# Delta-rule layer of a decoder trunk: the substitution's scratch, one tile for the lower blocks, and the place of the decays' product and the norms in GpSimd's queue

## The chip, the cores and the metric

The kernel runs on one core of a Trainium2 chip. A core has TensorE (matmuls; PE in the profile, PEld for its weight loads), VectorE (DVE), ScalarE (ACT), GpSimd (POOL) and SyncE (SP, which here only issues DMAs). Each engine runs its own queue of instructions in order; engines wait for one another through semaphores. The metric is the device time of one execution in microseconds, the median of several runs. A profiled execution is one run with the hardware profiler on; its page and its trace are what is quoted here.

## The reference

The program is a decoder trunk of four pre-norm residual layers (pooling mixer, gated DeltaNet, latent attention, pooling mixer) for 256 tokens and a model width of 1024, in float32. The change lies in the second layer, the delta rule. Cut to what matters:

```python
q = l2norm(q) * (GDN_DK ** -0.5);  k = l2norm(k)
g = cumsum(-exp(a_log) * softplus(a_raw + dt_bias))      # within a chunk
L = where(strict, (k_beta @ k.T) * decay, 0)
A = eye(C) + L
sol = triangular_solve(A, [v_beta, k_beta * exp(g)], lower=True)
attn = where(causal, (q @ k.T) * decay, 0)
for chunk in chunks:                                     # scan with a state
    v_new = u_c - w_c @ state
    o = (q_c * exp(g_c)) @ state + attn_c @ v_new
    state = state * exp(g_last) + k_dec.T @ v_new
o = rmsnorm(o, norm_g) * silu(gate)
```

There are 8 heads, keys of width 128 and values of width 256. The kernel takes chunks of 128 tokens instead of 64, so there are two (`NT` = 2).

## The kernel before

All large products run on TensorE from weights that are streamed from memory: SyncE loads a unit of a weight matrix into `raw` (line 104), ScalarE rounds it to the part `whi` (line 114), VectorE, or GpSimd for a few units, takes the difference `wlo` (line 119), and TensorE multiplies both with the activations (lines 128 to 130 and 169). This stream runs through the whole kernel and keeps TensorE busy; the rest of each layer is fitted beside it.

A framework traces the program, chooses the places of all tiles in the on-chip memory, plans the order of each engine's queue from a model of the durations, and sets the semaphores. Tiles of one tag (`s4` for the big ones) have no fixed places: a tile is put on bytes that an earlier tile has left, and its first writer then waits for that tile's last reader. `later(ins)` keeps what is traced inside it behind `ins` on the same engine's queue.

The delta layer's steps are listed by hand in line 561: `g0 k0 d a0 k1 a1 s g1 q0 v0 v1 v2 q1 V3 i c3 g2 u0 u1 g3`. In words: gates (`g`, the silu gate's projection), keys of four heads each (`k0`, `k1`), decays (`d`, exponentials of the tiles DT, Eb and eG), the lower-triangular blocks (`a`, into the two tiles `LT`), the substitution (`s`), queries (`q0`, `q1`), values (`v0` to `v3`; the fourth is split into its projection `V3` and its rest `c3`), the inverses (`i`) and the first chunk's new values (`u`).

The steps that matter:

- `substitution` (lines 717 to 751). The 32 by 32 diagonal blocks of `LT` (for 2 chunks, 8 heads and 4 blocks: 64 of them) are copied to DRAM by eight DMAs of SyncE's queue (line 723) and read back with one block on each of 64 partitions, `Lb` (line 728). GpSimd then solves all 64 at once, 31 pairs of a product into the scratch `pr` (line 733) and a difference into `Tb` (line 737). The result goes to DRAM (line 740) and back to the diagonal blocks of `T` by four DMAs of GpSimd's queue (line 744), each for one of the four blocks of all heads. VectorE and GpSimd also prepare factors here (lines 746 to 750).
- `queries(hf)` (lines 755 to 770). `channels` projects four heads, runs the short convolution (lines 635 and 638) and a silu into the tile `kqT`, that is `qT[hf]` (line 674), and turns it for the norms (line 680). `against` multiplies with the keys (line 693) and writes the masked scores (line 697). Then GpSimd multiplies the decays by the queries (`ev`, line 765) and computes the norms (lines 766 to 770); all of this stands in `later(mark["blocks"])`, and `mark["blocks"]` is the last difference of line 737.
- `inverses` (lines 806 to 857) stands in `later(mark["strip"], mark["dve"])` (line 881), that is behind the last matmul of `V3` on TensorE and behind the last split of a weight on VectorE. It turns the blocks T into the tiles `U` (line 817), reuses `Lb` and `Tb` as `X1` (memset in line 816), and combines blocks to full inverses in `pairs` (lines 826, 832) and `whole` (lines 840 to 853), four small batches of matmuls for each chunk. The first product of `pairs` (line 826) reads the first and the third block column of T (`blocks(T[t], 0)`).
- After that come `news` (line 867) and the outputs of each head (lines 892 to 956), which read the norms (lines 925 to 928).

Of the kernel before, what the change touches and what calls it, by code (L numbers as in the profile page):

```python
# [13 lines left out]
ALU = mybir.AluOpType  # L14
AX = mybir.AxisListType

P = 128
D = 1024
S = 256
NT = S // P  # L20
# [22 lines left out]
def trunk(ctx: ExitStack, tc: tile.TileContext, x, positions, norm_g, pool_w_in, pool_w_grp,  # L43
          pool_scale, pool_w_out, gdn_w_in, gdn_conv, gdn_a_log, gdn_dt_bias, gdn_norm_g,
          gdn_w_out, mla_w_in, mla_q_norm_g, mla_w_uq, mla_kv_norm_g, mla_w_ukv, mla_w_out,
          final_g, out, depth=4, final=True):
    nc = tc.nc
# [22 lines left out]
    def big(name, *dims, dt=F32):  # L70
        return s4.tile([P, *dims], dt, tag="s4", name=name)
# [7 lines left out]
    def small(name, *dims, bufs=2):  # L79
        return sm.tile([P, *dims], F32, tag=name, name=name, bufs=bufs)  # L80
# [12 lines left out]
    mark = {}  # L93
# [443 lines left out]
    def gdn_layer(i, j, hT):  # L537
        H = GDN_H
        M = NT * H
# [34 lines left out]
        for t in range(NT):  # L574
# [8 lines left out]
                                in1=dtb[:, None, :].to_broadcast([P, NT, H]))  # L583
# [13 lines left out]
                                in1=alog[:, None, :].to_broadcast([P, NT, H]))  # L597
# [14 lines left out]
        for t in range(NT):  # L612
            nc.gpsimd.dma_start(
                out=Gb[t].rearrange("p h s -> p (h s)"),
                in_=d_g[t * H:(t + 1) * H, :].rearrange("(a h) s -> a (h s)", a=1).to_broadcast(
                    [P, H * P]))
# [26 lines left out]
        Q, B = 4, 32  # L643
        Tb_ = big("Tb", B, B)
        Tb = Tb_[:M * Q]
        free = []
        nc.gpsimd.memset(Tb, 0.0)
        nc.gpsimd.memset(Tb.rearrange("m r c -> m (r c)")[:, ::B + 1], 1.0)
        Ts = big("T", NT, H, P)
# [4 lines left out]
        kT, qT = [], []  # L654
# [43 lines left out]
                    out=dst[t][:, h, :], in0=ps[:, b], scalar=sf[:, t, h:h + 1],  # L698
                    in1=DT[t][:, h, :], op0=ALU.mult, op1=ALU.mult)

        LT = [big("LT", H, P) for _ in range(NT)]

        def keys(hf):
            hs = slice(4 * hf, 4 * hf + 4)
# [8 lines left out]
        def lower(hf):  # L713
            for t in range(NT):
                against(LT, kT, s2, hf, t)

        def substitution():

            d_l = dram.tile([M * Q, B * B], F32, name="d_l")
            lv = d_l.rearrange("(t m d) (r c) -> t d r m c", t=NT, d=Q, r=B)  # L720
            for t in range(NT):
                for d in range(Q):
                    nc.sync.dma_start(out=lv[t, d],
                                      in_=LT[t][d * B:(d + 1) * B, :, d * B:(d + 1) * B])
            Lb_ = big("Lb", B, B)
            Lb = Lb_[:M * Q]
            free.extend((Lb_, Tb_))
            nc.sync.dma_start(out=Lb, in_=d_l.rearrange("m (r c) -> m r c", r=B))
            pr = small("pr", 256, bufs=1)[:M * Q]
            for r in range(B - 1):  # L730
                n, c = B - 1 - r, r + 1
                pv = pr[:, :n * c].rearrange("m (a b) -> m a b", a=n)
                nc.gpsimd.tensor_tensor(out=pv, op=ALU.mult,  # L733
                                        in0=Lb[:, r, r + 1:, None].to_broadcast([M * Q, n, c]),
                                        in1=Tb[:, r:r + 1, :c].to_broadcast([M * Q, n, c]))
                tv = Tb[:, r + 1:, :c]
                mark["blocks"] = nc.gpsimd.tensor_tensor(out=tv, in0=tv, in1=pv,  # L737
                                                         op=ALU.subtract).ins
            d_t = dram.tile([M * Q, B * B], F32, name="d_t")
            nc.gpsimd.dma_start(out=d_t.rearrange("m (r c) -> m r c", r=B), in_=Tb)  # L740
            tv = d_t.rearrange("(m d) (r c) -> d r m c", d=Q, r=B)
            for d in range(Q):
                dd = slice(d * B, (d + 1) * B)
                nc.gpsimd.dma_start(out=Ts[dd, :, :, dd].rearrange("p t h c -> p (t h) c"),
                                    in_=tv[d])
            nc.vector.reciprocal(rki, rk)
            nc.vector.tensor_tensor(out=kds, in0=rk[:, 0, :], in1=DT[0][:, :, P - 1],
                                    op=ALU.mult)
            nc.vector.tensor_scalar(neG, eG[:, 1, :], -1.0, None, ALU.mult)
            nc.gpsimd.tensor_tensor(out=ktok, in0=ktok, op=ALU.mult,  # L750
                                    in1=kds[:, :, None].to_broadcast([P, H, P]))
# [3 lines left out]
        def queries(hf):  # L755
            if hf == 0:
                at_.extend(big("attnT", H, P) for _ in range(NT))
            channels(qT, 0, hf, 1)
            for t in range(NT):
                against(at_, qT, rk, hf, t)  # L760
            ev = Eb[:, 4 * hf:4 * hf + 4, :]
            rh, qh = rq[:, :, 4 * hf:4 * hf + 4], rq2[:, :, 4 * hf:4 * hf + 4]

            with later(mark["blocks"]):
                nc.gpsimd.tensor_tensor(out=ev, in0=ev, in1=qT[hf][:, :, P:], op=ALU.mult)
                nc.gpsimd.tensor_scalar(qh, ssq[:, 1, :, 4 * hf:4 * hf + 4], float(P), EPS * P,
                                        ALU.mult, ALU.add)
                power(rh, qh)
                nc.gpsimd.tensor_tensor(out=qh, in0=rh, in1=rh, op=ALU.mult)
                nc.gpsimd.tensor_scalar(qh, qh, 1.0 / DV, None, ALU.mult)  # L770
# [29 lines left out]
            values_in(vi)  # L800
            values_done(vi)

        U = []
        u1 = []

        def inverses():
# [2 lines left out]

            U.extend(big("U", H, P) for _ in range(NT))

            X1 = [a.rearrange("p (h a) c -> p h (a c)", h=H) for a in free]
            for t in range(NT):
# [462 lines left out]
```

## Time and profile before

| | before |
|---|---|
| runs, us | 863.2, 864.64, 864.9 |
| median, us | 864.64 |
| profiled execution, us | 861.29 |
| its span, us | 859.5 |
| mean granted TensorE clock | 0.988 |
| DMA read from memory | 137.79 MB |

The span is the time between the first and the last instruction of the profiled execution; the 1.8 us around it are launch and end. The page gives for each engine how long it was busy, 40 slices of the span with the busy share of each engine, the granted TensorE clock in tenths of full speed, the DMA queues, the chain of work that ended last, and the costliest groups of instructions. The trace behind it can be asked for the instructions of an engine in order of time (start, duration, engine, line, operation, output and inputs, and in brackets how long the engine stood idle before it and what released it), for who waited for whom (total, times, longest, all in us), and for the busy time of each engine in stretches of the span.

### The profile page before, as it was taken

How to read it: one execution, taken by the hardware profiler on the slowest of the kernel's cores; microseconds unless marked ns; L12 is line 12 of the kernel's file. 1: busy time of each engine (PE TensorE's matmuls, PEld its weight loads, DVE VectorE, ACT ScalarE, POOL GpSimd, SP SyncE). 2: the span in 40 equal slices, each digit the busy share in tenths (PEclk: the TensorE clock that was granted, in tenths of full speed). 3: DMA queues.
4: the chain of work that ended last, by engine and by line, in shares of the span. 5: the costliest groups of instructions: out<-in, count | busy, mean ns of one | idle time of the engine just before them, and what ended most of it. 6: DMA issues, size and time to landing. Idle time of an engine off the chain costs nothing.

```text
span 859.5 us, 15387 instructions
## 1 busy us (share of the span) xinstructions
PE 834.2 (97%) x5967; PEld 780.0 (91%) x5967; DVE 568.4 (66%) x904; ACT 458.0 (53%) x757; POOL 168.5 (20%) x295
## 2 busy tenths in 40 slices
PE   7999999999999969999999999999999999999996
PEld 5999998979899968788989998999989979999986
DVE  4579866467889746355566557677767657766852
ACT  5555554466856634355455553566545465455542
POOL 4011000333338971022212003000000111100012
PEclk9999999999999979999999999999999999999999
DMA  5766657646556524303636676653552547566651
GB/s 196 228 197 192 203 171 224 193 122 205 168 172 194 172 76 144 124 26 104 190 108 220 203 174 191 172 149 97 151 171 80 159 148 217 182 188 183 205 184 50
DMA packets 109233, 140.37 MB, mean 163 GB/s; under 512 B 21228, under 2 KB 51112, under 8 KB 109160
## 3 DMA queue, kind: packets, MB, share of 16 engines
q1 hardware_dynamic: 106800, 137.65, 52.9%
q0 software_dynamic: 528, 1.58, 0.6%
q8 instruction: 47, 0.77, 0.4%
q10 hardware_dynamic: 1832, 0.16, 0.2%
q14 instruction: 26, 0.21, 0.1%
HBM read 137.79 MB, written 1.58 MB: 162 GB/s over the span
## 4 chain that ended last, share of the span: by engine, by line
PE 76%; POOL 7%; DMA 5%; DVE 5%; issue 3%; ACT 2%; SPq 0%; POOLq 0%; ACTq 0%; DVEq 0%
PE acc L169 32%; PE acc L130 10%; PE acc L129 10%; PE acc L128 10%; DMA raw<-in_pool_w_in_dram 3%; POOL pr L733 3%; POOL Tb L737 2%; PE aux L128 2%; PE aux L129 2%; PE aux L130 2%; DVE wlo L119 2%; ACT whi L114 1%; DMA raw<-in_mla_w_out_dram 1%; DVE cv L638 1%; PE aux L867 1%
## 5 line engine op out<-in xcount | busy, mean ns | idle before, releaser
L119 DVE TENSOR_TENSOR wlo<-raw,whi 128x1024 fp32r<-128x1024 f32 (+1 forms) x257 | 309.2, 1207 | 191.8 <-ACT whi L114 190.2
L114 ACT CAST whi<-raw 128x1024 fp32r<-128x1024 f32 (+2 forms) x258 | 265.3, 1032 | 245.8 <-PE acc L169 95.0
L129 PE MATMUL acc<-hTl,whi 128*128 128x256 f32 x832 | 235.1, 283 | 0.0
L130 PE MATMUL acc<-hTh,wlo 128*128 128x256 f32 x832 | 234.8, 283 | 0.0
L128 PE MATMUL acc<-hTh,whi 128*128 128x256 f32 x832 | 234.5, 282 | 0.0
L129 PEld LDWEIGHTS acc<-hTl,whi 128*128 128x128 f32 x832 | 158.7, 191 | 0.3
L128 PEld LDWEIGHTS acc<-hTh,whi 128*128 128x128 f32 x832 | 158.7, 191 | 0.4
L130 PEld LDWEIGHTS acc<-hTh,wlo 128*128 128x128 f32 x832 | 158.6, 191 | 0.1
L169 PE MATMUL acc<-wlo,yTh 128*128 128x256 f32 (+1 forms) x384 | 117.0, 319 | 0.0
L169 PE MATMUL acc<-whi,yTh 128*128 128x256 f32 (+1 forms) x384 | 115.8, 322 | 0.0
L169 PE MATMUL acc<-whi,yTl 128*128 128x256 f32 (+1 forms) x384 | 91.8, 320 | 0.0
L169 PEld LDWEIGHTS acc<-wlo,yTh 128*128 128x128 f32 x384 | 72.8, 190 | 5.0
L169 PEld LDWEIGHTS acc<-whi,yTh 128*128 128x128 f32 x384 | 72.1, 190 | 4.9
L169 PEld LDWEIGHTS acc<-whi,yTl 128*128 128x128 f32 x384 | 63.5, 190 | 5.1
L293 POOL TENSOR_TENSOR hg<-x,gain 128x256 f32<-128x256 f32 x18 | 14.7, 829 | 257.1 <-DVE x L355 254.2
L169 PE MATMUL acc<-wlo,hTh 128*128 128x512 f32 (+1 forms) x144 | 56.2, 392 | 2.5 <-DVE wlo L119 2.3
L169 PE MATMUL acc<-whi,hTh 128*128 128x512 f32 (+1 forms) x144 | 55.8, 394 | 0.7 <-ACT hTh L197 0.7
L169 PE MATMUL acc<-whi,hTl 128*128 128x512 f32 (+1 forms) x144 | 45.3, 388 | 0.1
L436 POOL COPY win<-u 128x4 f32<-128x4 f32 x8 | 6.1, 765 | 171.8 <-ACT u L430 171.8
L169 PEld LDWEIGHTS acc<-wlo,hTh 128*128 128x128 f32 x144 | 27.5, 191 | 9.1 <-DVE wlo L119 3.9
L169 PEld LDWEIGHTS acc<-whi,hTh 128*128 128x128 f32 x144 | 27.4, 190 | 7.0 <-ACT hTh L197 2.0
L169 PEld LDWEIGHTS acc<-whi,hTl 128*128 128x128 f32 x144 | 26.7, 190 | 5.6 <-DVE hTl L202 0.5
(342 smaller groups left out, 1451.9 us busy)
## 6 DMA issues: line engine op xcount, KB each, us to landing
raw<-in_pool_w_in_dram SPq DMA_DIRECT2D x60, 512.0 KB, 4.5
raw<-in_gdn_w_in_dram SPq DMA_DIRECT2D x48, 512.0 KB, 4.1
raw<-in_pool_w_out_dram SPq DMA_DIRECT2D x32, 512.0 KB, 3.8
raw<-in_mla_w_in_dram SPq DMA_DIRECT2D x24, 512.0 KB, 4.6
raw<-in_mla_w_uq_dram SPq DMA_DIRECT2D x36, 256.0 KB, 3.4
raw<-in_pool_w_grp_dram SPq DMA_DIRECT2D x16, 512.0 KB, 3.7
raw<-in_gdn_w_out_dram SPq DMA_DIRECT2D x16, 512.0 KB, 3.5
raw<-in_mla_w_ukv_dram SPq DMA_DIRECT2D x32, 256.0 KB, 3.4
```

Of the source, the lines that this page charges most:

```text
L114: a = nc.scalar.copy(hi[:, :m], raw[:, :m])
L119: b = e.tensor_tensor(out=lo[:, sl], in0=raw[:, sl], in1=hi.bitcast(F32)[:, sl], op=ALU.subtract)
L128: nc.tensor.matmul(o, lhsT=lhs[0], rhs=rhs[0], start=start, stop=False)
L129: nc.tensor.matmul(o, lhsT=lhs[0], rhs=rhs[1], start=False, stop=False)
L130: return nc.tensor.matmul(o, lhsT=lhs[1], rhs=rhs[0], start=False, stop=stop)
L169: nc.tensor.matmul(o, lhsT=act(k, t * P, P)[x], rhs=parts[j][z][:, sl], start=k == first and x == z == 0, stop=k == last and x == 1)
L293: nc.gpsimd.tensor_tensor(out=self.early[t, a], in0=xs[t][:, sl], in1=self.g[:, sl], op=ALU.mult)
L436: nc.gpsimd.tensor_copy(nxt[:, :, :d], cur[:, :, :d])
L638: nc.vector.scalar_tensor_tensor(out=o[:, d:], in0=ps[:, :S - d], scalar=tp(3 - d, c), in1=o[:, d:], op0=ALU.mult, op1=ALU.add)
L733: nc.gpsimd.tensor_tensor(out=pv, op=ALU.mult, in0=Lb[:, r, r + 1:, None].to_broadcast([M * Q, n, c]), in1=Tb[:, r:r + 1, :c].to_broadcast ...
L737: mark["blocks"] = nc.gpsimd.tensor_tensor(out=tv, in0=tv, in1=pv, op=ALU.subtract).ins
L867: nc.tensor.matmul(ps[:, c], lhsT=U[0][:, h, :], rhs=vR[h // 2][:, 0, c * DV:(c + 1) * DV], start=True, stop=True)
```

## The change

The diff does five things.

- The scratch `pr` of the substitution is no tile of its own any more: the two tiles `U` are taken in `substitution` instead of `inverses`, and `pr` is a view of `U[0]`.
- The two tiles `LT` become one tile `LTs` with two halves, and the eight DMAs of line 723 become four, each with both chunks.
- `mark["blocks"]` is the last of the four DMAs of line 744 instead of the last difference of line 737.
- The product of decays and queries (line 765) moves out of `later(mark["blocks"])`.
- The norms (lines 766 to 770) stay in it, and so stand behind the DMAs.

```diff
@@ -643,7 +643,7 @@
-        free = []
+        free, U = [], []
...
@@ -698,7 +698,8 @@
-        LT = [big("LT", H, P) for _ in range(NT)]
+        LTs = big("LT", NT, H, P)
+        LT = [LTs[:, t] for t in range(NT)]
...
@@ -717,16 +718,18 @@
             d_l = dram.tile([M * Q, B * B], F32, name="d_l")
-            lv = d_l.rearrange("(t m d) (r c) -> t d r m c", t=NT, d=Q, r=B)
-            for t in range(NT):
-                for d in range(Q):
-                    nc.sync.dma_start(out=lv[t, d],
-                                      in_=LT[t][d * B:(d + 1) * B, :, d * B:(d + 1) * B])
+            lv = d_l.rearrange("(m d) (r c) -> d r m c", d=Q, r=B)
+            for d in range(Q):
+                dd = slice(d * B, (d + 1) * B)
+                nc.sync.dma_start(out=lv[d],
+                                  in_=LTs[dd, :, :, dd].rearrange("p t h c -> p (t h) c"))
             Lb_ = big("Lb", B, B)
             Lb = Lb_[:M * Q]
             free.extend((Lb_, Tb_))
             nc.sync.dma_start(out=Lb, in_=d_l.rearrange("m (r c) -> m r c", r=B))
-            pr = small("pr", 256, bufs=1)[:M * Q]
+
+            U.extend(big("U", H, P) for _ in range(NT))
+            pr = U[0].rearrange("p h s -> p (h s)")[:M * Q, :256]
             for r in range(B - 1):
...
                 tv = Tb[:, r + 1:, :c]
-                mark["blocks"] = nc.gpsimd.tensor_tensor(out=tv, in0=tv, in1=pv,
-                                                         op=ALU.subtract).ins
+                nc.gpsimd.tensor_tensor(out=tv, in0=tv, in1=pv, op=ALU.subtract)
             d_t = dram.tile([M * Q, B * B], F32, name="d_t")
             nc.gpsimd.dma_start(out=d_t.rearrange("m (r c) -> m r c", r=B), in_=Tb)
             tv = d_t.rearrange("(m d) (r c) -> d r m c", d=Q, r=B)
             for d in range(Q):
                 dd = slice(d * B, (d + 1) * B)
-                nc.gpsimd.dma_start(out=Ts[dd, :, :, dd].rearrange("p t h c -> p (t h) c"),
-                                    in_=tv[d])
+                back = nc.gpsimd.dma_start(
+                    out=Ts[dd, :, :, dd].rearrange("p t h c -> p (t h) c"), in_=tv[d])
+            mark["blocks"] = back.ins
...
@@ -760,9 +763,9 @@
             ev = Eb[:, 4 * hf:4 * hf + 4, :]
             rh, qh = rq[:, :, 4 * hf:4 * hf + 4], rq2[:, :, 4 * hf:4 * hf + 4]
+            nc.gpsimd.tensor_tensor(out=ev, in0=ev, in1=qT[hf][:, :, P:], op=ALU.mult)
 
             with later(mark["blocks"]):
-                nc.gpsimd.tensor_tensor(out=ev, in0=ev, in1=qT[hf][:, :, P:], op=ALU.mult)
                 nc.gpsimd.tensor_scalar(qh, ssq[:, 1, :, 4 * hf:4 * hf + 4], float(P), EPS * P,
                                         ALU.mult, ALU.add)
                 power(rh, qh)
...
@@ -800,7 +803,6 @@
-        U = []
         u1 = []
 
         def inverses():
@@ -809,7 +811,6 @@
-            U.extend(big("U", H, P) for _ in range(NT))
 
             X1 = [a.rearrange("p (h a) c -> p h (a c)", h=H) for a in free]
```

## The prediction

> **What bounds the kernel now.** I read the page's header and engine table first, then the busy time in short windows, then the list of waits, then the timeline of each engine around the gap.
>
> ```profile
> span 859.5 us, 15387 instructions
> PE 834.2 (97%) x5967; PEld 780.0 (91%) x5967; DVE 568.4 (66%) x904; ACT 458.0 (53%) x757; POOL 168.5 (20%) x295
> 295.00:300.00 5.00, 5.00 (x44) 5.00 (x44) 4.47 (x9) 1.98 (x5) 4.53 (x7) 1.00 0.69 196
> 300.00:305.00 5.00, 0.47 (x4) 0.27 (x3) 0.00 (x0) 0.00 (x0) 4.14 (x12) 0.75 0.04 14
> 305.00:310.00 5.00, 2.27 (x11) 2.27 (x12) 1.36 (x3) 2.74 (x5) 4.68 (x8) 0.50 0.25 52
> 310.00:315.00 5.00, 5.00 (x34) 5.00 (x34) 2.12 (x4) 1.14 (x3) 4.16 (x7) 0.73 0.46 123
> 315.00:320.00 5.00, 5.00 (x46) 5.00 (x44) 2.83 (x3) 3.60 (x6) 2.96 (x4) 1.00 0.48 143
> ```
>
> The columns of a window are its length, the busy time (with instruction count) of PE, PEld, DVE, ACT and POOL, the granted TensorE clock, the DMA share and GB/s. TensorE is busy 97% of the span, so only its idle time and its slow time can be won. The delta-rule layer holds one big gap: from 300 to 308 nobody works but GpSimd, and the clock falls to 0.50 and stays low until the window from 310 to 315.
>
> ```profile
> ACT kqT L674 <- POOL Gb L765: 10.3, 1, 10.3
> PE tp L680 <- ACT kqT L674: 7.3, 1, 7.3
> DVE U L817 <- DMA T<-d_t: 5.0, 1, 5.0
> ...
> 258.81 0.23 POOL L733 TENSOR_TENSOR pr<-Lb,Tb 64x31 f32<-64x31 f32 x1 [11.47 <-DMA Lb<-d_l]
> ...
> 305.18 0.30 POOL L816 MEMSET Lb<- 128x256 f32 x1
> 305.45 0.23 POOL L733 TENSOR_TENSOR pr<-Lb,Tb 64x31 f32<-64x31 f32 x1
> 305.76 0.24 POOL L737 TENSOR_TENSOR Tb<-Tb,pr 64x31 f32<-64x31 f32 x1
> 305.97 1.26 POOL L765 TENSOR_TENSOR Gb<-Gb,kqT 128x512 f32<-128x512 f32 x1
> 307.31 0.20 POOL L766 TENSOR_SCALAR rq<-ssq 128x8 f32<-128x8 f32 x1
> 307.57 0.66 POOL L740 DMA_DIRECT2D d_t<-Tb  x1
> 308.24 1.68 POOL L662 TENSOR_TENSOR rq<-rq,halves 128x8 f32<-128x8 f32 x1
> 310.83 2.68 POOL L744 DMA_DIRECT2D T<-d_t  x4 [0.90 <-DMA d_t<-Tb]
> ...
> 307.26 0.42 ACT L674 ACTIVATE kqT<-cv 128x256 f32<-128x256 f32 x1 [10.28 <-POOL Gb L765]
> ```
>
> GpSimd's substitution runs from 258.81 to 306.00. Behind it stands L765, which reads the first query tile (`qT[0]`); the second (`qT[1]`, written by L674) lies on the first one's bytes in the planned layout. So ScalarE's L674 waits 10.3 us, until L765 ends at 307.23, and TensorE waits 7.3 us for L674. But behind the gap stands a second deadline:
>
> ```profile
> 300.07 0.28 PE L128 MATMUL acc<-hTh,whi 128*128 128x256 f32 x1
> 300.19 0.28 PE L129 MATMUL acc<-hTl,whi 128*128 128x256 f32 x1
> 307.73 0.69 PE L680 MATMUL tp<-ident,kqT 128*128 128x128 f32 x2 [7.25 <-ACT kqT L674]
> ...
> 309.28 0.41 PE L128 MATMUL acc<-hTh,whi 128*128 128x256 f32 x1
> 309.49 0.41 PE L129 MATMUL acc<-hTl,whi 128*128 128x256 f32 x1
> ...
> 318.57 1.90 PE L826 MATMUL aux<-T,LT 128*128 128x64 f32 x16
> 320.27 0.47 PE L169 MATMUL acc<-whi,hTh 128*128 128x512 f32 x1
> ...
> 317.18 2.37 DVE L817 STREAM_TRANSPOSE U<-T 128x1024 f32<-128x1024 f32 x2 [5.02 <-DMA T<-d_t]
> ```
>
> L826, the first step of the inverses, reads the solved blocks T, which come back through DRAM. VectorE waits for the last of T's four transfers until 317.18; TensorE reaches L826 at 318.57, 1.4 us later. The gap thus hides a wait for T nearly as long as itself.
>
> **The change, part by part.** The sum is made against the profiled execution (861.29 us: the span and 1.8 us around it); the median of the runs shown is 864.64, 3.35 more, and I add that at the end.
>
> *L765 for the first heads goes ahead.* It needs only `qT[0]` and the decays. In the order of before, the memset L816 stands between the last pairs of the substitution though it belongs to a later step: the planner lets whatever is ready into such a gap. So I place L765 a few pairs into the substitution, at 1.26 us (its row). `qT[1]` is then free long before L674, and the 7.25 us stall goes.
>
> What is late next? TensorE's work between L680 and L826 took 318.57 − 307.73 = 10.84 us, of it about 5.0 us (to 312.7) at half clock: starts 0.21 apart against 0.12 at full clock, so 5.0 × (1 − 0.12/0.21) = 2.2 us were lost. (A mean clock of 0.73 from 310 to 315 is 0.50 up to 312.7.) At full clock it is 8.6 us, and TensorE stands at L826 at 300.47 + 8.6 = 309.1. There T isn't landed. The inverses stay queued straight behind the projection V3 (line 881), and gate 2's matmuls (L169) stand behind L826, as do VectorE's, behind L817. So the stall moves; the question is when T lands.
>
> *The copies to DRAM, eight to four.*
>
> ```profile
> 245.47 2.16 DVE L697 SCALAR_TENSOR_TENSOR LT<-aux,s,DT 128x128 f32<-128x128 f32 x8
> ...
> 246.62 3.93 SPq L723 DMA_DIRECT2D d_l<-LT  x6
> 250.65 0.40 SPq L104 DMA_DIRECT2D raw<-in_gdn_w_in_dram  x1
> 251.09 0.96 SPq L723 DMA_DIRECT2D d_l<-LT  x2
> 252.15 0.40 SPq L104 DMA_DIRECT2D raw<-in_gdn_w_in_dram  x1
> 255.35 0.51 SPq L728 DMA_DIRECT2D Lb<-d_l  x1
> ...
> 255.96 0.72 ACT L674 ACTIVATE kqT<-cv 128x256 f32<-128x256 f32 x2
> ```
>
> The eight issues stretch from 246.62 to 252.05, with a weight load between them. Four issues, each for both halves of LT, can begin only when all of it is written (247.63). At 0.5 us each (the x2 row) they end at 249.7, 2.4 earlier; if each costs twice as much for twice the bytes, at 251.6, 0.4 earlier. The same 256 KB in the same short runs go out. I take 1.6 us, between 0 and 2.4. L765's input is written by 256.68, so it doesn't hold the substitution up.
>
> *GpSimd against VectorE.*
>
> ```profile
> 282.57 0.62 POOL L733 TENSOR_TENSOR pr<-Lb,Tb 64x256 f32<-64x256 f32 x1
> 284.09 1.50 POOL L733 TENSOR_TENSOR pr<-Lb,Tb 64x255 f32<-64x255 f32 x1
> 283.69 1.41 DVE L119 TENSOR_TENSOR wlo<-raw,whi 128x1024 fp32r<-128x1024 f32 x1
> ...
> 308.64 0.69 DVE L119 TENSOR_TENSOR wlo<-raw,whi 128x512 fp32r<-128x512 f32 x1 [9.13 <-ACT whi L114]
> 310.55 1.21 DVE L119 TENSOR_TENSOR wlo<-raw,whi 128x1024 fp32r<-128x1024 f32 x1
> ```
>
> The same GpSimd step takes 0.62 us alone and 1.50 beside VectorE's split of a weight (L119): 0.88 us a meeting. In before the last 6 us of the substitution ran beside an idle VectorE, because the stall held up the two splits at 308.64 and 310.55. Without the stall they fall into that tail: 2 × 0.88 = 1.8 us, between 0 and 1.8. An earlier start meets one more split at its head, 0.4 (0 to 0.88). The Trainium skill speaks against this change here: "SBUF — State Buffer", section "Who interferes with whom", says that a VectorE instruction with two SBUF inputs and a GpSimd instruction that reads SBUF exclude each other for the whole instruction. By that rule a meeting may cost the full split, 0.69 + 1.21 = 1.9 us for the two, against 1.8 by the rows; the sum goes by the rows.
>
> *L765 and the norms leave the way.* From the last L737 (ends 306.00) to L740 (307.57) 1.57 us go. L662, L769 and L770 now stand behind the last L744; in before L662 lay under the transfer for which L744 waited anyway, so nothing more comes of it. The norms are first read at 368.98, so what hides them is 50 us of other work; without it their 2.4 us would stand ahead of the outputs.
>
> ```profile
> 368.98 0.20 POOL L925 TENSOR_TENSOR oss<-oss,rq 128x2 f32<-128x2 f32 x1 [33.41 <-ACT junk L211]
> ```
> The other moves (scratch in `U[0]`, one tile LTs) change no instruction; U[0] lay on the scratch's bytes already, but its first writer L817 waits for T anyhow. I cost them at nothing; what a new layout does elsewhere is in the range.
>
> **The sum.** T moves by −1.6 + 0.4 + 1.26 + 1.8 − 1.57 = +0.3 us (bounds −2.7 to +3.2). What T's five transfers meet on the DMA engines changes too:
>
> ```profile
> DMA to landing us min/median/max: 2.5/4.4/5.1
> ```
>
> Between the median and the ends lie −1.9 and +0.7 us; I take 0, and the bounds become −4.6 and +3.9. L826 reads only the columns that the first and third of the four transfers bring; the fourth ends by 317.18, an issue takes 2.68/4 = 0.67, so its data was there at 316.5 (an estimate), and will be at 316.8. TensorE then waits from 309.1 to 316.8, and this 7.7 us gap is as long as the old one, so the clock falls again and the 2.2 us of slow matmuls come after L826 instead of ahead of it: 316.8 + 2.2 = 319.0 against 318.57. Forecast +0.4 us: 861.7 in the profiled execution, 865.0 in the median: **no change**. Break-even is a TensorE start at L826 of 318.57 − 2.2 = 316.4. "TensorE: Matmul & The Clock Gate", Part 1, of the Trainium skill gives a window of about 3.4 us for falling and for rising; by it the slow stretch would cost some 1.5 us, and the sum would be −0.3; the row's 5.0 us is used. ±0.2% (1.7 us) is about what a measurement of this kernel can tell from no change.
>
> **The rivals.**
>
> *T early (faster).* The copies save their 2.4 us and the splits miss the substitution: T moves by −2.4 + 1.26 − 1.57 = −2.7. L826 starts at 316.5 − 2.7 = 313.8; with 2.2 of slow time that counts as 316.0, 2.6 us faster: 862.1 in the median (860.2 if T's transfers also run at their shortest). For: four issues instead of eight are in the diff. Against: the rows of the meetings.
>
> *Gate 2 fills the wait (faster).* If the new plan puts gate 2's 48 matmuls ahead of L826, most of 7.25 + 2.2 = 9.5 us is won: 855.2. Against: the queue order of before has L826 directly behind V3, and nothing in the diff touches line 881.
>
> *The substitution pays (slower).* Place: GpSimd's queue. Price: L765 meets a split too (1.26 + 0.88), both late splits hit (1.8), one hits the head (0.88), and the start is not earlier (0): −1.57 + 2.1 + 1.8 + 0.9 = +3.2; L826 at 319.7, +2.2 = 321.9, 3.3 us slower, 868.0. It decides as soon as L826 starts later than 316.4 + 1.7.
>
> *The change doesn't do what it says.* The second query tile lands on other bytes that GpSimd holds, or the planner leaves L765 behind the substitution: the old gap stays and only L740 is earlier, which L826 doesn't notice: about 864.6.
>
> **How the numbers follow.** Stall moved, no change 0.38; not as said 0.07; T early 0.22; gate 2 fills 0.07; substitution pays 0.26. So faster 0.29, same 0.45, slower 0.26. The range leaves out gate 2's case and the ends of the others: 861.0 to 868.0.
>
> **What would show it.** L674's wait for L765 gone, and no TensorE gap at 300; instead one ahead of L826, 6 to 8 us long, ended by the DMA of T, with clock 0.50 behind it. L765 between two pairs of the substitution; steps near its end at 1.4 to 1.5 us beside L119; L733's first start some 1.6 us earlier. I am wrong if L169 stands between V3 and L826, if the clock doesn't fall, or if another stage of the 860 us moves by more than 1 us because of the new layout.

## The result, and the profile after

| | before | after |
|---|---|---|
| median of 7 runs each, us | 864.37 | 870.64 |
| lowest to highest, us | 861.18 to 865.96 | 869.34 to 874.17 |
| profiled execution, us | 861.29 | 874.15 |
| its span, us | 859.5 | 872.4 |
| mean granted TensorE clock | 0.988 | 0.98 |

The ratio of the medians is 1.0093 (95% interval 1.0067 to 1.0119): the changed kernel is slower by 0.9%, about 6 us in these runs, and lies above the predicted range. (In the changed kernel the lines behind the moved code stand one to three further down: L733 is L736, L737 is L740, L740 is L742, L744 is L746, L765 is L766, L817 and L826 are L818 and L827, L723 and L728 are L724 and L729.)

The predicted step did happen. First the page's header and engine table of the changed kernel, then its timeline around the substitution and the inverses (start, duration, engine, line, operation, output and inputs, count, and in brackets the idle time before it with what ended it):

```profile
span 872.4 us, 15379 instructions
PE 837.1 (96%) x5967; PEld 781.9 (90%) x5967; DVE 570.1 (65%) x904; ACT 459.3 (53%) x757; POOL 170.6 (20%) x295
```

```profile
267.56 0.23 POOL L736 TENSOR_TENSOR U<-Lb,Tb 64x31 f32<-64x31 f32 x1 [17.59 <-DMA Lb<-d_l]
...
270.13 1.29 POOL L766 TENSOR_TENSOR Gb<-Gb,kqT 128x512 f32<-128x512 f32 x1
...
317.58 0.24 POOL L740 TENSOR_TENSOR Tb<-Tb,U 64x31 f32<-64x31 f32 x1
318.12 0.64 POOL L742 DMA_DIRECT2D d_t<-Tb  x1 [0.29 <-POOL Tb L740]
321.36 2.65 POOL L746 DMA_DIRECT2D T<-d_t  x4 [2.60 <-DMA d_t<-Tb]
325.28 3.65 PE L827 MATMUL aux<-T,LT 128*128 128x64 f32 x16 [6.05 <-DMA T<-d_t]
```

L766 now runs inside the substitution, 2.6 us after its start, and TensorE no longer waits for L674. It waits 6.05 us at L827 for T instead. But the whole scene is late: the substitution starts at 267.56 where it started at 258.81, and that is 8.75 us, while the prediction had it 1.6 us earlier.

To place the time I cut the span of each profile at the same steps. The numbers are the lengths of the stages in us, worked out from the start of the named instruction in each trace (layer 1 includes the launch; a norm is L298):

```
stage                                            before   after   after, run again
layer 1, up to the first norm of layer 2         171.32  173.07   170.95
... to the first pair of the substitution         87.49   94.49    92.26
... to the issue of the copy d_t                  48.76   50.56    51.12
... to the first matmul of the inverses (L826)    11.00    7.16     7.15
... to the first new values (L867)                38.37   41.99    42.05
... to the first norm of layer 3                  72.06   71.53    72.88
... to the first norm of layer 4                 260.54  264.90   264.98
... to the last sum (L355)                       163.33  162.34   162.07
```

The first stage differs between executions of one and the same kernel (169.6 to 173.1 us in the fourteen profiles of this case) and says nothing. The rows that count are four. The wait at the inverses is 3.8 us shorter and the stage behind it 3.6 us longer, which nearly cancels, as the prediction had it. The way to the substitution is 4.8 to 7.0 us longer, and layer 3, which the change does not touch, 4.4 us longer, of which the last stage gives 1.0 to 1.3 back.

Where the way to the substitution lost its time, the windows of busy time show. Before, then after (columns as in the prediction: start and end, length, busy time of PE, PEld, DVE, ACT, POOL, clock, DMA share, GB/s):

```profile
235.00:265.00 30.00, 29.47 (x248) 29.18 (x248) 27.51 (x62) 17.57 (x29) 12.25 (x17) 1.00 0.60 177
265.00:300.00 35.00, 35.00 (x297) 35.00 (x296) 31.33 (x51) 22.55 (x40) 32.10 (x38) 1.00 0.61 179
```

```profile
235.00:265.00 30.00, 24.79 (x205) 24.21 (x204) 26.07 (x52) 13.22 (x20) 8.56 (x6) 1.00 0.54 156
265.00:300.00 35.00, 33.28 (x269) 33.08 (x268) 29.71 (x56) 22.65 (x42) 29.62 (x39) 0.95 0.52 155
```

TensorE, which had lost 0.5 us in these 65 us, now loses 5.2 and 1.7. The list of waits of the changed kernel from 225 to 300 us (engine, line, what it waited for: us in total, times, longest) and the timeline of SyncE's queue:

```profile
POOL U L736 <- DMA Lb<-d_l: 17.6, 1, 17.6
ACT whi L114 <- DMA raw<-in_gdn_w_in_dram: 13.2, 7, 5.0
PE acc L128 <- DVE cv L638: 5.2, 3, 2.1
```

```profile
248.91 0.37 SPq L104 DMA_DIRECT2D raw<-in_gdn_w_in_dram  x1
253.08 0.34 SPq L724 DMA_DIRECT2D d_l<-LT  x1
253.51 1.37 SPq L104 DMA_DIRECT2D raw<-in_gdn_w_in_dram  x1
254.93 0.99 SPq L724 DMA_DIRECT2D d_l<-LT  x2
256.02 0.55 SPq L104 DMA_DIRECT2D raw<-in_gdn_w_in_dram  x1
256.61 0.51 SPq L724 DMA_DIRECT2D d_l<-LT  x1
257.22 4.26 SPq L104 DMA_DIRECT2D raw<-in_gdn_w_in_dram  x2
261.77 0.52 SPq L729 DMA_DIRECT2D Lb<-d_l  x1
```

SyncE's queue runs in order. It comes to the first of the four copies at 249.28 and stands there for 3.8 us, because that copy needs both halves of LT. Four weight loads stand behind or between the copies in this list and are issued late. ScalarE waits 13.2 us for weights in these 75 us (1.9 us in before), 5.0 of it for the first load behind the copies. TensorE itself waits each time for a convolution step of VectorE (L638), the 5.2 us in three pieces: 1.26 us at 237.21, ahead of the copies, 1.80 at 250.44 and 2.15 at 261.60. Only the third comes from the weights: VectorE's split at 259.83 waits for ScalarE's rounding of that load, and the convolution step stands behind the split. The second comes from VectorE's own order. Its timeline in the changed kernel:

```profile
246.63 2.21 DVE L119 TENSOR_TENSOR wlo<-raw,whi 128x512 fp32r<-128x512 f32 x1
248.76 1.22 DVE L711 TENSOR_TENSOR s<-s,rk 128x8 f32<-128x8 f32 x1
...
250.90 2.15 DVE L697 SCALAR_TENSOR_TENSOR LT<-aux,s,DT 128x128 f32<-128x128 f32 x8
...
259.83 1.23 DVE L119 TENSOR_TENSOR wlo<-raw,whi 128x1024 fp32r<-128x1024 f32 x1 [2.44 <-ACT whi L114]
260.98 0.47 DVE L638 SCALAR_TENSOR_TENSOR cv<-acc,tap,cv 128x253 f32<-128x253 f32 x1
```

The last blocks of LT are written until 253.05, against 247.63 in before. Two splits (L119) and two steps of a convolution (L638) now stand between the preparation L749/L750 and these blocks; in before there were none. No line of the diff is about VectorE; the planner ordered the queue anew.

The lost 7.0 us of this stage can be read at its events, counted from the first norm of layer 2. LT is written 3.7 us later than in before (at 79.98 us instead of 76.31). The issues of the copies behind it take 0.4 us less. What follows, the copies' landing and the reading back of `Lb` with weight loads issued in between, takes 3.7 us more: 4.65 us instead of 3.29 from the end of the last issue to the issue of `Lb`, and 5.79 instead of 3.46 from there to the first pair. Run again, the three parts are +2.9, −0.8 and +2.7 us.

### The profile page after: what moved, and what is told of

Read it like the earlier page. It is cut to its first block, busy times and chain, and to the rows that moved or that the text cites. A ratio compares the mean times of both kernels' runs of the same rounds, so it can differ in the third digit from the quotient of the medians.

```text
span 872.4 us, 15379 instructions
## 1 busy us (share of the span) xinstructions
PE 837.1 (96%) x5967; PEld 781.9 (90%) x5967; DVE 570.1 (65%) x904; ACT 459.3 (53%) x757; POOL 170.6 (20%) x295
## 4 chain that ended last, share of the span: by engine, by line
PE 71%; DMA 8%; POOL 7%; DVE 7%; ACT 3%; issue 3%; SPq 1%; ACTq 0%; POOLq 0%; DVEq 0%
PE acc L169 30%; PE acc L128 9%; PE acc L129 9%; PE acc L130 9%; DMA raw<-in_pool_w_in_dram 3%; POOL Tb L740 3%; POOL U L736 2%; DVE wlo L119 2%; PE aux L128 2%; PE aux L129 2%; PE aux L130 2%; ACT whi L114 2%; DVE cv L638 1%; DMA Gb<-d_g 1%; DMA x<-in_x_dram 1%
## 5 line engine op out<-in xcount | busy, mean ns | idle before, releaser
L119 DVE TENSOR_TENSOR wlo<-raw,whi 128x1024 fp32r<-128x1024 f32 (+1 forms) x257 | 308.0, 1203 | 185.3 <-ACT whi L114 184.2
```

Of the source, the lines that this page charges most:

```text
L119: b = e.tensor_tensor(out=lo[:, sl], in0=raw[:, sl], in1=hi.bitcast(F32)[:, sl], op=ALU.subtract)
```

## The experiments

Each median is beside that of the kernel before on the same chip. In the edits, "before" and "changed" name the kernel that the edit starts from.

### The copies: four, eight, and from which queue

The first theory: the four copies cause the loss, and the rest of the change costs little. The rival: the new place of L766 and of the norms, or the layout, costs it. Two kernels separate them. The first does the copies' part alone, from before:

```diff
-        LT = [big("LT", H, P) for _ in range(NT)]
+        LTs = big("LT", NT, H, P)
+        LT = [LTs[:, t] for t in range(NT)]
...
-            for t in range(NT):
-                for d in range(Q):
-                    nc.sync.dma_start(out=lv[t, d],
-                                      in_=LT[t][d * B:(d + 1) * B, :, d * B:(d + 1) * B])
+            for d in range(Q):
+                dd = slice(d * B, (d + 1) * B)
+                nc.sync.dma_start(out=lv[d],
+                                  in_=LTs[dd, :, :, dd].rearrange("p t h c -> p (t h) c"))
```

> The kernel before with only the one tile LTs and the four copies. Theory A (the four copies make the planner put other work ahead of the last blocks of LT in VectorE's queue, and weight loads behind the waiting copies in SP's): LT full at about 253 us instead of 247.6, substitution starts at 265 to 269 instead of 258.8, TensorE under 5.0 of 5 us in several windows from 235 to 265; the decays' product still stands behind the substitution, so the stall at L674 stays; 868 to 874 us in the median, 4 to 9 above the kernel before. Theory B (the early decays' product or the early U re-plans the queues, not the copies): substitution starts before 260, 863 to 865 us. Theory C (the prediction's): four issues are shorter, start 257 to 259, 862 to 865 us.

Measured: 870.19 us beside 862.11, ratio 1.0089 (1.0067 to 1.0111). It has the whole loss without any of GpSimd's moves, and its stages show it in the same two places: 92.79 us to the substitution and 265.05 in layer 3.

The second is the changed kernel with the old loop of eight copies out of the one tile.

> The changed kernel with eight copies from the one tile, as before; all else as changed. Theory A: LT full at 247 to 249 us, substitution starts at 258 to 260, L766 inside it, the wait ahead of L827 about 8 us long and ending near 318; 864 to 867 us (the prediction's sum with the copies' term at 0 is T +1.9 us). Theory B: the start stays above 264 and the time at 869 to 874 us.

Measured: 859.87 us beside 862.11, ratio 0.9972 (0.996 to 0.9985), faster than before and below what either theory expected. From 235 to 265 us TensorE is busy all the time, and the substitution starts at 258.02. The window and the timeline of this kernel:

```profile
235.00:265.00 30.00, 30.00 (x254) 29.81 (x253) 23.23 (x53) 16.45 (x28) 13.12 (x18) 1.00 0.57 174
```

```profile
244.22 2.16 DVE L697 SCALAR_TENSOR_TENSOR LT<-aux,s,DT 128x128 f32<-128x128 f32 x8
245.37 4.10 SPq L724 DMA_DIRECT2D d_l<-LT  x6
250.05 0.96 SPq L724 DMA_DIRECT2D d_l<-LT  x2
...
258.02 0.96 POOL L736 TENSOR_TENSOR U<-Lb,Tb 64x31 f32<-64x31 f32 x1 [11.92 <-DMA Lb<-d_l]
```

The copies begin at 245.37, while the second half of LT is still being written, as they did in before; nothing in SyncE's queue waits long. So it is the four copies, but their number alone or the queue in which they stand? The next kernel keeps the four and moves them to GpSimd's queue, which holds no weight loads:

```diff
-                nc.sync.dma_start(out=lv[d],
+                nc.gpsimd.dma_start(out=lv[d],
```

> The changed kernel with the four copies issued from GpSimd's queue, which stands idle there, instead of SP's; the planner then leaves VectorE's order as it was before. Theory A (the four copies cost nothing by themselves; what costs is their place among the weight loads in SP's queue and the order of VectorE that is planned with them): LT full at 246 to 249 us, the substitution starts at 254 to 260, TensorE full from 245 to 265; 856 to 862 us. Rival (copies of both chunks are late or slow in themselves): start after 263 us, 866 to 873 us.

Measured: 862.80 us beside 862.54, ratio 1.0006 (0.9988 to 1.0024). In its timeline:

```profile
249.16 2.71 POOL L724 DMA_DIRECT2D d_l<-LT  x4 [0.58 <-DVE LT L697]
255.95 0.52 SPq L729 DMA_DIRECT2D Lb<-d_l  x1
261.52 0.23 POOL L736 TENSOR_TENSOR U<-Lb,Tb 64x31 f32<-64x31 f32 x1 [9.65 <-DMA Lb<-d_l]
```

TensorE is busy 29.47 us from 235 to 265, as in before; VectorE writes LT in its old place; layer 3 takes 259.62 us. The time is a little above the theory's range, and most of the loss has gone with the copies still four: +0.3 us against before, where the four on SyncE's queue cost +6.3 to +8.6 and the eight gained 2.2. So some 2.5 us stay with the four copies, wherever they are issued. In the stage they show behind the last issue: from its end to the first pair it takes 9.65 us here and 6.75 in before, 9.5 to 10.4 in the five profiles with four copies and 6.7 to 7.4 in the nine with eight. How much of this is the landing of the larger copies, and how much the weight loads that SyncE's queue issues in between, was not tried apart.

The issues themselves are no dearer for twice the bytes: two take 0.99 us in SyncE's queue of the changed kernel and 0.96 in before. On GpSimd's queue one takes 2.71/4 = 0.68 us.

Layer 3 shows the same split: 264.9 to 265.1 us in the three runs with four copies on SyncE's queue, 260.5 in before, 259.2 with eight copies from one tile. At the start of layer 4 TensorE waits 2.5 to 2.7 us for L310 in those three, and 0 to 0.9 us in the eleven other profiles. First the list of waits and the windows of the changed kernel, then the window of before around the same step, which starts there at 690.70:

```profile
PE tp L325 <- ACT h L310: 2.5, 1, 2.5
...
700.00:705.00 5.00, 2.47 (x21) 2.27 (x20) 2.49 (x5) 1.73 (x6) 2.95 (x6) 0.92 0.73 218
705.00:710.00 5.00, 5.00 (x16) 3.95 (x17) 3.92 (x7) 4.33 (x8) 0.98 (x3) 0.50 0.01 2
```

```profile
685.00:695.00 10.00, 9.76 (x70) 8.81 (x68) 5.65 (x11) 6.04 (x18) 6.47 (x13) 1.00 0.42 122
```

And the last sums of layer 3 on VectorE, in the changed kernel and in the one with eight copies:

```profile
687.78 1.29 DVE L355 TENSOR_TENSOR x<-acc,x 128x512 f32<-128x512 f32 x2 [1.52 <-PE acc L169]
700.71 1.08 DVE L355 TENSOR_TENSOR x<-acc,x 128x256 f32<-128x256 f32 x3
```

```profile
686.38 0.77 DVE L355 TENSOR_TENSOR x<-acc,x 128x256 f32<-128x256 f32 x2
688.88 0.42 DVE L355 TENSOR_TENSOR x<-acc,x 128x256 f32<-128x256 f32 x1 [1.73 <-PE acc L169]
691.04 0.42 DVE L355 TENSOR_TENSOR x<-acc,x 128x256 f32<-128x256 f32 x1 [0.17 <-PE acc L169]
```

The last product of the layer has four parts, two for each half of the tokens. With eight copies TensorE's queue finishes them one after another, 18 matmuls each. The two parts of the first 128 tokens are added at 686.38, their norm follows 3 us later, and TensorE has the matmuls of the other two parts beside it and never stands. With four copies the matmuls of three parts are interleaved in TensorE's queue: the three are added together at 700.71, 13 us behind the last sum, the norm follows 3 us later as well, but only the fourth part's 18 matmuls are left beside it. TensorE waits 2.5 us, and its clock falls to 0.50. That is another order of the same work, planned 440 us behind the edit. Why the planner chooses it was not found.

The changed kernel was also run once more as it is:

> The changed kernel once more, for a second trace beside those of the experiments. If the four copies' cost lies in the queues that are planned with them, the same stages are long again: the substitution starts 94 to 95 us after the first norm of the second layer (87.5 before), the norms at the end of the third layer come 264 to 265 us after those at its start (260.5 before), with three of the last sums of line 355 together and TensorE waiting 2 to 3 us at L325. The first layer's 171 to 173 us, where the queues are as before, may come out either way if its length is chance from one execution to the next. 868 to 872 us in the median. If the late stages of the first trace were a disturbance: 866 us or less.

Measured: 870.95 us beside 862.35, ratio 1.0092 (1.0069 to 1.0114). Its stages stand in the table above; TensorE is busy 26.48 us from 235 to 265 and waits 2.6 us at L325. So the two places repeat, the first with 4.8 instead of 7.0 us.

### The decays' product alone

Does moving L765 by itself free the second query tile, as the prediction had it? From before, that line is moved out of `later(mark["blocks"])` and nothing else:

```diff
+            nc.gpsimd.tensor_tensor(out=ev, in0=ev, in1=qT[hf][:, :, P:], op=ALU.mult)

             with later(mark["blocks"]):
-                nc.gpsimd.tensor_tensor(out=ev, in0=ev, in1=qT[hf][:, :, P:], op=ALU.mult)
```

> The kernel before with only the decays' product moved ahead of the substitution's end (the norms stay ahead of the copies of T). Theory A: start at 258 to 260 us, no stall at L674, a wait of TensorE ahead of L826 of about 8 us in its place, T about 1 to 3 us later than before: 864 to 867 us. Theory B: substitution starts after 264, 869 us or more. If a stall of TensorE could simply be removed: 855 us.

Measured: 862.63 us beside 862.11, ratio 1.0005 (0.9992 to 1.0019). The stall stays; its list of waits:

```profile
ACT kqT L674 <- POOL Tb L737: 9.9, 1, 9.9
```

L674 now waits for L737, the substitution itself, until its end: in this kernel's layout the second query tile lies on the bytes of the scratch `pr`. The time fits neither theory, since no stall has moved and none has gone. So the rival "the change doesn't do what it says" is what L765 alone gives. In the changed kernel, with the scratch in `U[0]` and the tiles `U` taken early, L674 waits for nothing of GpSimd's.

### One tile or two: the places

The kernel with eight copies was faster than before although it still has the wait at the inverses. One theory: the norms behind T's transfers bring that. To try it, before was given the scratch in `U[0]` and L765 ahead, with two tiles, eight copies, and the norms behind the last difference, as they were:

```diff
-            pr = small("pr", 256, bufs=1)[:M * Q]
+            U.extend(big("U", H, P) for _ in range(NT))
+            pr = U[0].rearrange("p h s -> p (h s)")[:M * Q, :256]
...
+            nc.gpsimd.tensor_tensor(out=ev, in0=ev, in1=qT[hf][:, :, P:], op=ALU.mult)
```

> As e2_eight_again, with two tiles LT and with the mark for the norms as before (the last difference instead of the last copy of T), so that norms stand ahead of the copies. By the prediction's step one short norm (0.2 us and its gaps, 0.3 us) stands ahead of the first copy and the others lie under the transfer for which GpSimd waits anyhow: T 0.3 us later, 860 to 861 us, not to be told from e2_eight_again. Rival (moving the norms behind is what gained): 862 us or more.

Measured: 865.54 us beside 862.54, ratio 1.0034 (1.0018 to 1.0049). With the norms moved back it should have stayed ahead of before, and it is 3.0 us behind; the 5.2 us between −2.2 and +3.0 are more than the norms' 2.4 us of GpSimd's time. Two more kernels took the tile and the norms apart: before with the one tile `LTs` and nothing else (eight copies out of its halves), and the changed kernel with two tiles and eight copies.

> The kernel before with only the one tile LTs (eight copies, all else as before): every engine's queue stands in the same order as before, only places of tiles differ. Theory P (place): in e2_eight_again the matmuls with hTh and hTl of the second half of the tokens follow each other at 0.114 us in the third and fourth layer, where before and e8_norms_ahead show 0.120, and these tiles lie elsewhere in the planned layout; 528 such matmuls there times 0.006 is 3.2 us, and some 1.5 more in the first layer. So 857 to 860 us, 2.5 to 5 below before, with substitution and stall at L674 unchanged. Rival (e2_eight_again is faster by its delta layer or by chance): 861.5 to 863.5 us, the same as before.

> As e2_eight_again but with two tiles LT; the queues stand in the same order, only places differ. Theory P: spacing 0.120 in the later layers, 863 to 866 us, as e8_norms_ahead, whose norms then cost nothing. Rival (in e8_norms_ahead the norms ahead of the copies of T cost the 5 us): 859 to 861 us, as e2_eight_again.

Measured: the tile alone 859.14 us beside 862.78, ratio 0.9955 (0.9938 to 0.9971); the two tiles 864.77, ratio 1.0019 (1.0005 to 1.0033). So it is the tile that is worth about 3.6 us, and the norms' place that is worth little. The kernel with the tile alone has the same instructions in the same order as before on all five queues; places in the on-chip memory differ and, with them, three semaphore waits in layers 3 and 4. Where its time goes, two windows show, each around one strip of 48 matmuls in layer 4. Each of these matmuls takes all 256 tokens. The first strip is on the first half of the 1024 channels, the second on the second half, and this is what the expectation calls the second half of the tokens. Before, then the tile alone:

```profile
757.20:762.66 5.46, 5.46 (x51) 5.46 (x49) 2.94 (x3) 2.68 (x4) 0.00 (x0) 1.00 0.56 170
762.66:768.40 5.74, 5.74 (x50) 5.74 (x49) 2.45 (x2) 2.61 (x3) 0.00 (x0) 1.00 0.62 197
```

```profile
756.56:762.00 5.44, 5.44 (x50) 5.44 (x49) 3.25 (x3) 2.72 (x4) 0.00 (x0) 1.00 0.55 152
762.00:767.44 5.44, 5.44 (x50) 5.44 (x49) 2.45 (x2) 2.59 (x3) 0.00 (x0) 1.00 0.68 220
```

TensorE has no idle time in either window and the granted clock is 1.00, but the second strip takes 5.74 us in before and 5.44 with the one tile. In the compiled layout the second half's activations (`hTh` and `hTl`, 4 KB each) of layers 1, 3 and 4 begin at 64.2 and 76.2 KB of a partition in before and at 24.1 and 28.1 KB with the one tile; the first half's begin at 16.1 and 20.1 KB in both. There are 864 matmuls on the second half in the three layers, 18 strips, so at most 18 × 0.30 = 5.4 us. In the profile of the tile alone 11 of the 18 strips run at 0.113 us a matmul and 7 at 0.118, where all 18 of before run at 0.120. By the means of each layer the second half gains 3.9 us and the first half loses 0.5, together 3.4; the measured gain is 3.6 us (2.5 to 5.3 by the ends of the ratio).

### The wait at the inverses

The prediction's rival that would win 9.5 us was gate 2's matmuls in the wait for T. With the copies back to eight, the order of steps was changed by hand:

```diff
-        order = "g0 k0 d a0 k1 a1 s g1 q0 v0 v1 v2 q1 V3 i c3 g2 u0 u1 g3".split()
+        order = "g0 k0 d a0 k1 a1 s g1 q0 v0 v1 v2 q1 V3 c3 g2 i u0 u1 g3".split()
```

> As e2_eight_again, with the order list changed to V3 c3 g2 i u0 u1 g3, so that the 48 matmuls of gate 2 stand ahead of L827. If the wait for T is the bound as the prediction has it: the 48 matmuls (about 11 us) cover the wait, TensorE gap ahead of L827 under 2 us, no fall of the clock there; 6 to 9 us won against e2_eight_again (857 to 861 us), less what the later steps of the inverses lose with gate 2 gone from between them. Rival (gate 2 is needed there): TensorE waits between L841, L845 and L851 instead, 5 us or more in all, and the time is within 2 us of e2_eight_again or above it.

Measured: 863.37 us beside 862.11, ratio 1.0020 (1.0002 to 1.0038), slower than the same kernel in the old order. Its timeline:

```profile
314.34 1.26 POOL L119 TENSOR_TENSOR wlo<-raw,whi 128x512 fp32r<-128x512 f32 x1
315.65 0.80 PE L169 MATMUL acc<-wlo,hTh 128*128 128x512 f32 x1 [4.92 <-POOL wlo L119]
```

One of gate 2's splits is GpSimd's, and stands in its queue behind the substitution. So TensorE waits for the same engine in another place. The next kernel gives gate 2's two splits to VectorE:

```diff
-                            pool=((0, 4), (7,), (3, 7), (7,))[vi])
+                            pool=((0, 4), (7,), (), (7,))[vi])
```

> As e4_gate_fills (eight copies, gate 2 ahead of the inverses), with none of gate 2's weight splits on GpSimd. If what spoiled e4_gate_fills is that its matmuls wait for splits that stand behind the substitution's copies in GpSimd's queue: no wait of TensorE for GpSimd's split, 48 matmuls done at about 318 us, L827 there at once (T landed at 316), no fall of the clock at 310 to 320; 3 to 7 us below e2_eight_again: 853 to 857 us. Rival (gate 2 is needed between the inverses' later steps): the waits come back at L841 to L868, 859 to 863 us.

Measured: 861.44 us beside 862.54, ratio 0.9991 (0.9975 to 1.0007). TensorE now comes to L827 without a wait, but it is not faster than with the gap. The waits of TensorE from 295 to 400 us in this kernel:

```profile
PE acc L169 <- DVE wlo L119: 2.6, 1, 2.6
PE tp L796 <- ACT vc L792: 2.4, 1, 2.4
PE aux L851 <- DVE X L848: 2.0, 2, 1.2
```

The one gap, 7.80 us in the kernel with eight copies and the old order, has become several of 0.3 to 2.6 us, 7.9 us in all: the first for VectorE's extra splits, the second in the rest of the values (L796), the others inside the inverses, whose small batches wait for one another and had gate 2 as filler. The fourth kernel has both this and the four copies on GpSimd's queue:

> The four copies from GpSimd's queue and gate 2 ahead of the inverses with its splits on VectorE. If both theories hold the gains add: at least as fast as e6_vector_splits, 852 to 857 us. If TensorE at L827 is no longer late once gate 2 covers the wait, an earlier T gives nothing more: the same as e6_vector_splits within 1.5 us.

Measured: 862.05 us beside 862.54, ratio 1.0004 (0.9984 to 1.0025): nothing.

### Eight copies from two queues

T's way still sets when the inverses begin. The last kernel leaves the first chunk's four copies in SyncE's queue and issues the second's from GpSimd's, at the same time:

```diff
-                    nc.sync.dma_start(out=lv[t, d],
+                    (nc.gpsimd if t else nc.sync).dma_start(out=lv[t, d],
```

> As e2_eight_again, with the four copies of the second chunk issued from GpSimd's queue beside SP's four of the first. If the issues are what holds the substitution's start: the last copy is issued 1.5 to 2 us earlier, the substitution starts 1 to 2 us earlier relative to the end of LT, L827 likewise: 858 to 859.5 us. Rival (the copies' landing is the bound): start within 0.5 us of e2_eight_again after the end of LT; 859 to 861 us.

Measured: 857.89 us beside 862.78, ratio 0.9945 (0.993 to 0.996). It beats before by 4.9 us and is the fastest of all. Its timeline:

```profile
245.66 1.82 SPq L724 DMA_DIRECT2D d_l<-LT  x4
246.97 2.43 POOL L724 DMA_DIRECT2D d_l<-LT  x4 [0.58 <-DVE LT L697]
...
256.82 0.96 POOL L736 TENSOR_TENSOR U<-Lb,Tb 64x31 f32<-64x31 f32 x1 [7.42 <-DMA Lb<-d_l]
```

The last copy is issued by 249.40, 2.7 us after LT is written, where the kernel with eight copies on one queue took until 251.01, 4.6 us after. The stage to the substitution is 1.5 us shorter (86.48 against 87.96 us). The Trainium skill, "DMA: Bandwidth & Descriptors", section "Issuing engines are not separate DMA queues", says that issuing from several engines saves only the time of the issuing sequencer; the rows agree, 1.9 us of issue time and no more, and here this is on the path that sets the end. The other 1.2 us of the difference between −4.9 and −2.2 are not explained; the planner ordered other stages a little differently too.

## Why the prediction was wrong, step by step

The ledger, each term relative to its own runs of before:

| part | us | from |
|---|---|---|
| one tile, same queues | −3.6 | the tile alone |
| GpSimd's moves: scratch, L765, norms | +2.0 | two tiles, eight copies: 864.77 − 862.78 |
| four copies on SyncE's queue | +11 | +8.1 − (−3.6) = +11.7 by the copies' part alone; +8.6 − (−2.2) = +10.8 by the changed kernel against the same with eight |
| sum | +9.4 | measured: +8.6 (run again), +6.3 (first runs) |

- **The failed step: "The copies to DRAM, eight to four".** The prediction let the substitution start 1.6 us earlier (0 to 2.4). It started 4.8 to 7.0 us later by its stage, and layer 3 was 4.4 us longer. The step counted the issues, at durations that were right (0.5 us each), and left every other instruction, and the transfers, as they had been. But four copies that each need both halves are another graph for the planner. VectorE's last blocks moved behind two splits, so that LT was written 2.9 to 3.7 us later; the copies moved in front of weight loads, so that a queue that runs in order passed the wait on to the weights; and the way from the last issue to the first pair took 2.7 to 3.7 us longer, for which there was no term ("The same 256 KB in the same short runs go out"). The prediction even wrote that the copies can begin only when all of LT is written, and did not ask what stands behind the first of them on SyncE's queue. That the copies in SyncE's queue are the cause is shown: they alone bring the loss, without them it is gone, and with them on GpSimd's queue most of it is gone. How much of it VectorE's order costs, and how much SyncE's, was not tried apart. Layer 3 is the sign of being wrong that the prediction named (another stage moves by more than 1 us), but not by the layout: there the order of the queues differs.
- **Mis-sized: "The other moves … I cost them at nothing".** The one tile is worth −3.6 us, through places alone. "What a new layout does elsewhere" was named as a doubt, without a price. It is on the opposite side of the error, so that without it the miss would have been larger.
- **Right: L765 into the substitution, and the norms behind.** The sum for the stage from the first pair to the copy d_t was +0.4 + 1.26 + 1.8 − 1.57 = +1.9 us; the stages are longer by 1.8 us in the changed kernel, 2.4 when run again and 2.0 in the changed kernel with eight copies. That the sum is right does not show each term. Two steps of the changed kernel's tail are long beside a split of VectorE, 0.96 us at 309.44 and 1.35 at 312.17, but the meetings were not tried alone.
- **Right in kind, off in size: "So the stall moves".** The gap ahead of the inverses is there and ends with T's DMA, 6.05 us long where 7.7 was expected, since T's way back from the issue of d_t took 7.2 us, not 8.9. The prediction put T's transfers at no change, with −1.9 as the lower bound; they came out near that bound. The clock fell as expected, and TensorE worked longer at the low clock, which takes it back:

```profile
325.00:332.00 7.00, 6.72 (x24) 6.08 (x25) 6.20 (x14) 2.52 (x5) 6.09 (x7) 0.50 0.28 80
```

  From 325.28 the granted clock is 0.50 for nearly 7 us, where the stretch of before had 5.0. The Trainium skill, "TensorE: Matmul & The Clock Gate", Part 1, has a window of about 3.4 us for the clock to rise again. The trace agrees with the window and not with one being enough: the clock is low for 10.24 us in both kernels, three times 3.41 (302.47 to 312.71 and 321.94 to 332.18), and every low stretch of the fourteen profiles between 20 and 800 us is a whole number of such windows long. In before the first whole window of work, from 309.30, is the last low one. In the changed kernel the first, from 325.35, does not end it; it holds the small matmuls of L827. Why it doesn't count is open, and where the windows fall against the gap is chance.

  Stage by stage: −3.8 us ahead of L827 and +3.6 behind it, against −2.1 and +2.2 in the prediction. So −0.2 where it had +0.1: two errors that cancel, which is luck. The kernel with two tiles and eight copies, which has only these terms and not the copies, came out at +2.0 us (0.4 to 2.8 by the ends of the ratio); the prediction's own terms without the copies' −1.6 make that +2.0 as well.
- **The rival "Gate 2 fills the wait"** had the wrong price. Its 9.5 us took the gap as free time to be filled; in the runs with gate 2 moved by hand the filled gap came back as waits for splits and inside the inverses, and the gain was nothing.
- **The rival that ended on the slower side** put its place in GpSimd's queue and reached 868.0. The loss was larger, and in SyncE's and VectorE's queues. A part of the condition is in the rows of before, where weight loads stand between the copies on SyncE's queue; the new order of VectorE is not.

## What to carry to other kernels

Before a DMA is merged with another, ask what its later start keeps waiting behind it on its issuing queue, and how long the way to its first reader then is. On a queue that also streams weights it was better here to leave the transfer split (−2.2 us) or to issue it elsewhere (+0.3) than to let it wait there (+6.3 to +8.6). Where a planner orders the queues, a change of the graph can move work that no line of the diff names, so the order of all queues, in other stages too, is to be compared before a loss is explained by the edit itself. A wait that hides another can be priced only with the second deadline and with what the filler was covering.

## What the hardware showed that was not expected

The pace of matmuls goes with the place of the moving operand. At a granted clock of 1.00, with no idle time in the windows above, matmuls of 256 columns follow each other every 5.74/48 = 0.120 us when their activations begin at 64.2 and 76.2 KB of a partition and every 5.44/48 = 0.113 us at 24.1 and 28.1 KB. It was so in all fourteen profiles: in layers 1, 3 and 4 the second half's strips run at 0.120 in the four kernels with two tiles, every one of the 18, and at 0.113 or 0.118, strip by strip, in the ten with one. In layer 2 the activations lie at 64 KB and above in either layout, and there both halves run at 0.120 in every profile. What makes the difference, the address itself or what else then uses that part of the memory, stays open, and so does why some strips at the low places take 0.118.
